# Retention with two heads per pair: products in alternating head order, and head factors by transposes

## The chip, the cores and the metric

The kernel runs on one core of one Trainium2 chip. The metric is device time in microseconds (us) from launch to end; lower is better. A core has TensorE (PE, matrix products; its weight loads are shown as PEld), VectorE (DVE), ScalarE (ACT), GpSimd (POOL) and SyncE (SP, which here issues nearly all DMA transfers). TensorE reads SBUF and writes PSUM, which has eight banks.

## The reference, cut to what matters

Two layers, each a token mixer with four branches (retention, short convolution, Fourier, pooling) and then a SwiGLU block, on 256 latent tokens; layer 0 also carries 256 context tokens as a second stream. Everything is float32. The part that the change touches is the retention, with 4 heads of 64 features:

```python
scores = jnp.einsum('bhid,bhjd->bhij', qc, kc) * intra[None]
out = (jnp.einsum('bhij,bhjv->bhiv', scores, vc)
       + jnp.einsum('bhid,bhdv->bhiv', qc, state) * q_decay)
state = state * chunk_decay + jnp.einsum('bhjd,bhjv->bhdv', kc * k_decay, vc)
...
mu = jnp.mean(y, axis=-1, keepdims=True)
var = jnp.mean(jnp.square(y - mu), axis=-1, keepdims=True)
y = (y - mu) * lax.rsqrt(var + EPS)
```

It runs forward and backward over the tokens; the context's final states are the start states of the latent stream. Each head's output is normalized over its 64 features and multiplied by a gate.

## The kernel before

All large projections are done in three float32r products per block (`mm3`, L208 to L212: high part times high part, and the two mixed ones). The weights come block by block through SyncE's queue; ScalarE copies the high part of each (L105) and VectorE subtracts it to get the low part (L115). The schedule is written out by hand: a list of steps is run in order, and after a step that holds a block, `tick` (L216) lets up to two of the queued side jobs go on by one `yield`. Retention is such a side job: TensorE works on a projection, then does one small burst for retention, then goes on with the next projection.

`retention(c)` (L741) handles the pair of heads 2c and 2c+1, for c = 0 and then c = 1, once in each layer: four times in all. Head j of the pair has its 64 features in partitions `off[j]`, 0 to 63 or 64 to 127. Its stages, one burst on TensorE each:

- L749, L750: SyncE loads `qd` (decay factors of q) and `dm` (decay masks).
- L753, `ktp`: the context's keys are transposed, 2 transposes per pair.
- L766 to L775, `st`: the states at the end of the context; per head two products of 128 rows, 64 columns and 128 moving columns into the head's half of one PSUM bank.
- L783 to L792, `scores`: per head two products of 64 rows (the head's features) and 256 moving columns into a bank of its own; then VectorE multiplies by the mask (`am`, L791).
- L799 to L804, `heads`: `py`, one bank, where head j writes partitions `off[j]`. Two products per head with `am` (128 rows, 64 columns), and for the latent stream (`s == 0`) two more with the states (`st` times `qd`, 64 rows, 64 columns).
- L806, L807: ScalarE squares `py`, VectorE multiplies it by the gate.
- L810 to L821, `variance`: VectorE and POOL make the norm's factor per token and head, and VectorE copies it out to 64 columns per head (`rx`, L820).
- L827, `normed`: `rx` (tokens by features) is brought to features by tokens by a float32 product with the identity, two per stream; VectorE multiplies (L829), and ScalarE and VectorE split the result into high and low part for the gates' products.

In layer 0 (NS = 2) scores and heads run first for the context (s = 1), then for the latent stream (s = 0); layer 1 has s = 0 alone. So the program has four `st` sets, six `scores` sets, two `heads` sets without states (s = 1) and four with (s = 0). In the program, each set lists all products of head 0 and then all of head 1. The banks of tag "a" that these stages use go round in order (L177).

Of the kernel before, what the change touches and what calls it, by code (L numbers as in the profile page):

```python
# [12 lines left out]
ALU = mybir.AluOpType  # L13
# [4 lines left out]
P = 128  # L18
D = 1024
KC = D // P  # L20
SEQ = 256
MIX = 256
HEADS = 4
DH = 64
# [135 lines left out]
def kernel(ctx: ExitStack, tc: tile.TileContext, a: dict, out: bass.AP):  # L160
    ctx.enter_context(tc.manual_schedule())
    nc = tc.nc
# [14 lines left out]
    def bank(tag, name, shape=None, keep=False):  # L177

        i = banks[tag].pop(0)
        if not keep:  # L180
            banks[tag].append(i)
        t = psum.tile([P, 512], F32, tag=f"bank{i}", name=name)
        return t if shape is None else cut(t, shape)
# [4 lines left out]
    def cut(t, shape):  # L188
        n = 1
        for x in shape:  # L190
            n *= x
        t = t[:, :n]
        if len(shape) == 2:
            t = t.rearrange("p (a b) -> p a b", b=shape[1])
        if len(shape) == 3:
            t = t.rearrange("p (a b c) -> p a b c", b=shape[1], c=shape[2])
        return t

    def load(pl, shape, src, name, eng=None, **kw):
        t = pl.tile(shape, F32, name=name, **kw)  # L200
        (eng or nc.sync).dma_start(t, src)
        return t

    def split(hi, lo, src):
        nc.scalar.activation(hi, src, AF.Copy)
        nc.vector.tensor_tensor(lo, src, hi.bitcast(F32), op=ALU.subtract)
# [24 lines left out]
    ident = load(cst, [P, P], a["c_ident"], "ident", nc.scalar)  # L231
# [375 lines left out]
    def mixer(l, h, hnext, start=None):  # L607
# [8 lines left out]
        def rt(tag, shape, name, bufs=1):  # L616
            n = 1
            for x in shape:
                n *= x
            return cut(P_["t"].tile([P, n], F32, tag=tag, name=name, bufs=bufs), shape)  # L620
# [5 lines left out]
        vt = []  # L626
# [105 lines left out]
        def both():  # L732
            yield from retention(0)
            yield
            yield from retention(1)

        def vrow(i, hh, at, dims):
            row = vscr[i][l * HEADS + hh : l * HEADS + hh + 1, 0:1]
            return bass.AP(row.tensor, row.offset + at, dims)

        def retention(c):  # L741

            kT, qT, gs, kt = qk["k", c], qk["q", c], qk["g", c], fix["kt"]
            off = [slice(j * DH, (j + 1) * DH) for j in range(2)]
            qd = rt("qd", [2, SEQ], f"qd{l}{c}")
            dm = [rt(f"dm{j}", [2, SEQ], f"dm{l}{c}{j}") for j in range(2)]
            for j in range(2):
                for d in range(2):
                    nc.sync.dma_start(qd[off[j], d, :], vrow(0, 2 * c + j, 257 * (1 - d), [[0, DH], [1, SEQ]]))  # L749
                nc.sync.dma_start(dm[j], vrow(1, 2 * c + j, 1, [[1, P], [P, 2], [1, SEQ]]))  # L750
            pt = bank("a", f"ktp{l}{c}", [2, P])
            for t in range(2):
                nc.tensor.transpose(pt[:, t, :], kT[:, (t + 2) * P : (t + 3) * P], ident)  # L753
            nc.scalar.activation(kt[:, :, c * P : (c + 1) * P], pt, AF.Copy)
            vd = rt("vd", [2, 2, 2 * DH], f"vd{l}{c}")
            for t in range(2):
                for d in range(2):
                    nc.vector.tensor_tensor(
                        vd[:, t, :, d * DH : (d + 1) * DH],
                        vt[1][:, t, 2 * c : 2 * c + 2, :],  # L760
                        kdec[:, l, t, d, 2 * c : 2 * c + 2].unsqueeze(2).to_broadcast([P, 2, DH]),
                        op=ALU.mult,
                    )
            yield
            pst = bank("a", f"st{l}{c}", [2 * DH])
            for j in range(2):  # L766
                hh = 2 * c + j
                for t in range(2):
                    nc.tensor.matmul(
                        pst[off[j], :],  # L770
                        lhsT=kt[:, t, hh * DH : (hh + 1) * DH],
                        rhs=vd[:, t, j, :],
                        start=(t == 0),
                        stop=(t == 1),
                    )  # L775
            st = rt("st", [2 * DH], "st")
            nc.scalar.activation(st, pst, AF.Copy)
            nc.vector.tensor_tensor(qd, qd, qT[:, :SEQ].unsqueeze(1).to_broadcast([P, 2, SEQ]), op=ALU.mult)

            def scores(s):  # L780
                sl = slice(s * SEQ, (s + 1) * SEQ)
                am = []
                for j in range(2):  # L783
                    pss = bank("a", f"sc{l}{c}{s}{j}", [2, SEQ])
                    for jt in range(2):
                        lo = s * SEQ + jt * P
                        nc.tensor.matmul(
                            pss[:, jt, :], lhsT=kT[off[j], lo : lo + P], rhs=qT[off[j], sl], start=True, stop=True
                        )
                    m = rt("am", [2, SEQ], "am", 3)  # L790
                    nc.vector.tensor_tensor(m, pss, dm[j][:, :, ::-1], op=ALU.mult)  # L791
                    am.append(m)  # L792
                return am

            def heads(s, am):
                sl = slice(s * SEQ, (s + 1) * SEQ)
                py = bank("a", f"y{l}{c}{s}")[:, :SEQ]
                n = 4 if s == 0 else 2
                for j in range(2):  # L799
                    todo = [(vt[s][:, jt, 2 * c + j, :], am[j][:, jt, :]) for jt in range(2)]  # L800
                    if s == 0:
                        todo += [(st[off[j], d * DH : (d + 1) * DH], qd[off[j], d, :]) for d in range(2)]
                    for i, (lhs, rhs) in enumerate(todo):
                        nc.tensor.matmul(py[off[j], :], lhsT=lhs, rhs=rhs, start=(i == 0), stop=(i == n - 1))  # L804
                ys = rt("ys", [2, SEQ], "ys", 2)
                nc.scalar.activation(ys[:, 0, :], py, AF.Square)  # L806
                nc.vector.tensor_tensor(ys[:, 1, :], py, gs[:, sl], op=ALU.mult)  # L807
                return ys

            def variance(s, ys):  # L810
                pv = bank("a", f"var{l}{c}{s}", [2, 2])
                for t in range(2):
                    nc.tensor.matmul(
                        pv[:, t, :], lhsT=ys[:, 0, t * P : (t + 1) * P], rhs=bsel, start=True, stop=True
                    )
                ms = sm.tile([P, 4], F32, tag="vms", name="vms")
                nc.vector.tensor_scalar(ms, pv.rearrange("p a b -> p (a b)"), EPS, None, op0=ALU.add)
                nc.gpsimd.tensor_tensor(ms, ms, mhalf, op=ALU.pow)
                rx = rt("rx", [4, DH], "rx", 2)
                nc.vector.tensor_copy(rx, ms.unsqueeze(2).to_broadcast([P, 4, DH]))  # L820
                return rx.rearrange("p a d -> p (a d)")  # L821

            def normed(s, ys, rx):
                pr = bank("a", f"yr{l}{c}{s}")[:, :SEQ]
                for t in range(2):
                    ts = slice(t * P, (t + 1) * P)
                    nc.tensor.matmul(pr[:, ts], lhsT=rx[:, ts], rhs=ident, start=True, stop=True)  # L827
                gy = ys[:, 1, :]
                nc.vector.tensor_tensor(gy, gy, pr, op=ALU.mult)  # L829
                sl = slice(s * SEQ, (s + 1) * SEQ)  # L830
                split(br[0][0][c][:, sl], br[0][1][c][:, sl], gy)

            yield
            am = {}
            for s in range(NS - 1, -1, -1):
                am[s] = scores(s)
                yield
                am[s] = heads(s, am[s])
                yield
            rx = {s: variance(s, am[s]) for s in am}  # L840
            yield
            for s in am:
                normed(s, am[s], rx[s])
# [589 lines left out]
    start = next(i for i, st in enumerate(mix0) if st.tick)  # L1433
# [123 lines left out]
```

## Time and profile before

| | us |
|---|---|
| median of 3 runs | 1261.3 (1260.61 to 1261.71) |
| profiled execution, as timed | 1262.2 |
| its span, first to last instruction | 1260.3 |
| TensorE busy in the span | 1222.6 (97%) |
| VectorE busy | 776.7 (62%) |
| ScalarE busy | 454.1 (36%) |
| POOL busy | 41.1 (3%) |

How to read it: the rows further down come from one profiled execution, so sums are made against its span. A float32 product shows as two matmul records (two passes), a float32r product and a transpose as one. Matmuls are pipelined and the ends of their records are modelled, so records overlap; the cost of a burst is read from the chain of waits or from start to start. "a\*b" in a matmul's row is its rows and columns in the array.

### The profile page before, as it was taken

What the parts mean: (1) busy time and instruction counts of PE and PEld (TensorE: products, weight loads), DVE (VectorE), ACT (ScalarE), POOL (GpSimd) and SP (SyncE); (2) the same over time, 40 slices, a digit from 0 to 9 for tenths busy, and PEclk for the clock granted to TensorE, in tenths of its full rate; (3) what the DMA queues carried; (4) which work ended last, traced back from release to release, by engine and by line L of the source; (5) the groups of instructions that cost most, each with busy time, mean ns of one, the idle gap of its engine ahead of it and who ended that gap; (6) DMA issues with size and microseconds to landing.
All of it is one profiled execution on the core that took longest, in us unless ns stands there. A gap on an engine that the chain in (4) does not pass through costs nothing.

```text
span 1260.3 us, 17305 instructions
## 1 busy us (share of the span) xinstructions
PE 1222.6 (97%) x6830; PEld 1044.5 (83%) x6830; DVE 776.7 (62%) x1242; ACT 454.1 (36%) x712; POOL 41.1 (3%) x39
## 2 busy tenths in 40 slices
PE   8999999999989989999999999989999999999997
PEld 4687878888878778888888788779889998999986
DVE  4453454399977465997666422475666666666644
ACT  3332332322222363222222222354334455444532
POOL 1500000000000000000000000000000000000000
PEclk9999999999999999999999999999999999999999
DMA  8542322566676424677768733244355564665672
GB/s 294 184 130 69 100 84 101 200 198 225 217 171 137 134 98 123 225 230 234 240 217 205 177 103 101 67 132 134 103 151 168 190 217 134 186 183 185 192 222 88
DMA packets 66434, 206.31 MB, mean 164 GB/s; under 512 B 14640, under 2 KB 18224, under 8 KB 66352
## 3 DMA queue, kind: packets, MB, share of 16 engines
q1 hardware_dynamic: 65200, 204.96, 52.7%
q8 instruction: 54, 0.88, 0.3%
q10 hardware_dynamic: 1152, 0.24, 0.1%
q14 instruction: 28, 0.23, 0.1%
HBM read 204.06 MB, written 1.11 MB: 163 GB/s over the span
## 4 chain that ended last, share of the span: by engine, by line
PE 81%; DVE 8%; ACT 3%; DMA 3%; issue 3%; POOL 0%; SPq 0%; ACTq 0%; DVEq 0%; POOLq 0%
PE up L211 10%; PE up L210 10%; PE up L212 10%; PE gate L210 5%; PE gate L211 5%; PE gate L212 5%; PE dn L212 4%; PE dn L211 4%; PE dn L210 4%; DVE mjunk L320 2%; PE y L804 1%; PE wo L212 1%; PE wo L211 1%; PE wo L210 1%; ACT junk L425 1%
## 5 line engine op out<-in xcount | busy, mean ns | idle before, releaser
L320 DVE SCALAR_TENSOR_TENSOR mjunk<-raw_mod,crow 128x1024 bf16<-128x1024 f32 x128 | 156.4, 1222 | 8.1 <-DMA raw_mod<-in_w_modt 5.5
L211 PE MATMUL up<-hm0lo,hi_up 128*128 128x512 f32 (+1 forms) x384 | 143.2, 373 | 0.4 <-DVE hm0lo L452 0.4
L210 PE MATMUL up<-hm0hi,hi_up 128*128 128x512 f32 (+1 forms) x384 | 143.3, 373 | 0.0
L212 PE MATMUL up<-hm0hi,lo_up 128*128 128x512 f32 (+1 forms) x384 | 143.2, 373 | 0.0
L115 DVE TENSOR_TENSOR lo_up<-raw_up,hi_up 128x1024 fp32r<-128x1024 f32 x88 | 107.5, 1223 | 34.0 <-ACT hi_up L105 34.0
L115 DVE TENSOR_TENSOR lo_gt<-raw_gt,hi_gt 128x1280 fp32r<-128x1280 f32 x64 | 95.3, 1488 | 33.6 <-ACT hi_gt L105 33.5
L115 DVE TENSOR_TENSOR lo_dn<-raw_dn,hi_dn 128x1024 fp32r<-128x1024 f32 x44 | 53.6, 1224 | 89.4 <-ACT hi_dn L105 89.4
L210 PE MATMUL gate<-h0hi,hi_gt 128*128 128x512 f32 x256 | 101.2, 395 | 4.0 <-DVE sg L989 3.9
L105 ACT ACTIVATE hi_gt<-raw_gt 128x1280 fp32r<-128x1280 f32 x64 | 81.1, 1268 | 54.0 <-DMA raw_gt<-in_w_gate 53.8
L211 PE MATMUL gate<-h0lo,hi_gt 128*128 128x512 f32 x256 | 100.4, 392 | 0.0
L210 PE MATMUL up<-hm1hi,hi_up 128*128 128x256 f32 x352 | 100.4, 285 | 0.0
L212 PE MATMUL gate<-h0hi,lo_gt 128*128 128x512 f32 x256 | 100.3, 392 | 0.0
L211 PE MATMUL up<-hm1lo,hi_up 128*128 128x256 f32 x352 | 100.3, 285 | 0.0
L212 PE MATMUL up<-hm1hi,lo_up 128*128 128x256 f32 x352 | 100.1, 284 | 0.0
L105 ACT ACTIVATE hi_up<-raw_up 128x1024 fp32r<-128x1024 f32 x88 | 92.2, 1049 | 14.4 <-DMA raw_up<-in_w_up 13.8
L211 PEld LDWEIGHTS up<-hm0lo,hi_up 128*128 128x128 f32 x384 | 72.9, 190 | 13.0 <-DVE hm0lo L452 0.6
L212 PEld LDWEIGHTS up<-hm0hi,lo_up 128*128 128x128 f32 x384 | 72.8, 190 | 12.7
L210 PEld LDWEIGHTS up<-hm0hi,hi_up 128*128 128x128 f32 x384 | 73.0, 190 | 12.5
L105 ACT ACTIVATE hi_dn<-raw_dn 128x1024 fp32r<-128x1024 f32 x44 | 46.3, 1057 | 93.5 <-PE dn L212 78.4
L210 PE MATMUL gate<-hf0hi,hi_gt 128*128 128x256 f32 x256 | 73.4, 287 | 0.0
L212 PE MATMUL gate<-hf0hi,lo_gt 128*128 128x256 f32 x256 | 72.4, 283 | 0.0
L211 PE MATMUL gate<-hf0lo,hi_gt 128*128 128x256 f32 x256 | 72.4, 283 | 0.0
(330 smaller groups left out, 2749.4 us busy)
## 6 DMA issues: line engine op xcount, KB each, us to landing
raw_up<-in_w_up SPq DMA_DIRECT2D x88, 512.0 KB, 3.9
raw_gt<-in_w_gate SPq DMA_DIRECT2D x64, 640.0 KB, 4.0
raw_mod<-in_w_modt SPq DMA_DIRECT2D x80, 512.0 KB, 4.0
raw_dn<-in_w_down SPq DMA_DIRECT2D x44, 512.0 KB, 3.7
raw_in<-in_w_in SPq DMA_DIRECT2D x28, 512.0 KB, 3.7
raw_mod<-in_w_mod SPq DMA_DIRECT2D x16, 512.0 KB, 4.6
raw_wo<-in_w_o SPq DMA_DIRECT2D x16, 512.0 KB, 4.1
grow<-gscr SPq DMA_DIRECT2D x6, 512.0 KB, 13.0
```

Of the source, the lines that this page charges most:

```text
L105: self.nc.scalar.activation(b.hi, b.raw, AF.Copy)
L115: self.nc.vector.tensor_tensor(b.lo, b.raw, b.hi.bitcast(F32), op=ALU.subtract)
L210: nc.tensor.matmul(ps, lhsT=st[0], rhs=mv[0], start=first, stop=False)
L211: nc.tensor.matmul(ps, lhsT=st[0], rhs=mv[1], start=False, stop=False)
L212: nc.tensor.matmul(ps, lhsT=st[1], rhs=mv[0], start=False, stop=last)
L320: nc.vector.scalar_tensor_tensor(junk, b.raw, 1.0, crow[s], op0=ALU.mult, op1=ALU.mult, accum_out=out()[:, s, i : i + 1])
L425: nc.scalar.activation(junk, src, AF.Square, scale=1.0 / 32.0, accum_out=acc)
L804: nc.tensor.matmul(py[off[j], :], lhsT=lhs, rhs=rhs, start=(i == 0), stop=(i == n - 1))
```

## The change

In three places the loop over the two heads goes inside the loop over their products, so that the products of head 0 and head 1 alternate: the states (`st`), the scores and `heads`. In `scores` both heads' banks are taken before the first product, and both masks are applied after the last. In `heads` the index i runs over the two products with `am` and, for the latent stream, the two with the states. The number of these products, their operands and the order of accumulation within a head stay the same. In `normed` the product with the identity is replaced by TensorE's transpose, as in L753. Nothing else changes.

```diff
             pst = bank("a", f"st{l}{c}", [2 * DH])
-            for j in range(2):
-                hh = 2 * c + j
-                for t in range(2):
+            for t in range(2):
+                for j in range(2):
+                    hh = 2 * c + j
                     nc.tensor.matmul(
                         pst[off[j], :],
...
                 am = []
+                pss = [bank("a", f"sc{l}{c}{s}{j}", [2, SEQ]) for j in range(2)]
+                for jt in range(2):
+                    lo = s * SEQ + jt * P
+                    for j in range(2):
+                        nc.tensor.matmul(
+                            pss[j][:, jt, :], lhsT=kT[off[j], lo : lo + P], rhs=qT[off[j], sl], start=True, stop=True
+                        )
                 for j in range(2):
-                    pss = bank("a", f"sc{l}{c}{s}{j}", [2, SEQ])
-                    for jt in range(2):
-                        lo = s * SEQ + jt * P
-                        nc.tensor.matmul(
-                            pss[:, jt, :], lhsT=kT[off[j], lo : lo + P], rhs=qT[off[j], sl], start=True, stop=True
-                        )
                     m = rt("am", [2, SEQ], "am", 3)
-                    nc.vector.tensor_tensor(m, pss, dm[j][:, :, ::-1], op=ALU.mult)
+                    nc.vector.tensor_tensor(m, pss[j], dm[j][:, :, ::-1], op=ALU.mult)
                     am.append(m)
...
                 n = 4 if s == 0 else 2
-                for j in range(2):
-                    todo = [(vt[s][:, jt, 2 * c + j, :], am[j][:, jt, :]) for jt in range(2)]
-                    if s == 0:
-                        todo += [(st[off[j], d * DH : (d + 1) * DH], qd[off[j], d, :]) for d in range(2)]
-                    for i, (lhs, rhs) in enumerate(todo):
+                for i in range(n):
+                    for j in range(2):
+                        if i < 2:
+                            lhs, rhs = vt[s][:, i, 2 * c + j, :], am[j][:, i, :]
+                        else:
+                            lhs, rhs = st[off[j], (i - 2) * DH : (i - 1) * DH], qd[off[j], i - 2, :]
                         nc.tensor.matmul(py[off[j], :], lhsT=lhs, rhs=rhs, start=(i == 0), stop=(i == n - 1))
...
                     ts = slice(t * P, (t + 1) * P)
-                    nc.tensor.matmul(pr[:, ts], lhsT=rx[:, ts], rhs=ident, start=True, stop=True)
+                    nc.tensor.transpose(pr[:, ts], rx[:, ts], ident)
```

## Rows read from the trace of the kernel before

**Rows 1.** The page, part 1 (busy us, share, instructions) and part 2 (granted clock by slices).

```profile
PE 1222.6 (97%) x6830; PEld 1044.5 (83%) x6830; DVE 776.7 (62%) x1242; ACT 454.1 (36%) x712; POOL 41.1 (3%) x39
...
PEclk9999999999999999999999999999999999999999
```

**Rows 2.** Stretches: length, busy PE, PEld, DVE, ACT, POOL, clock, DMA share, GB/s.

```profile
70.00:215.00 145.00, 145.00 (x703) 114.32 (x703) 72.38 (x124) 43.48 (x68) 4.03 (x4) 1.00 0.32 93
...
250.00:360.00 110.00, 109.89 (x485) 90.67 (x484) 106.83 (x156) 30.47 (x35) 0.00 (x0) 1.00 0.65 205
...
937.00:960.00 23.00, 23.00 (x177) 20.89 (x176) 14.64 (x23) 10.68 (x15) 1.01 (x1) 1.00 0.50 169
```

**Rows 3.** Waits of PE, 885 to 960 us: us in total, times, longest.

```profile
PE yr L827 <- DVE rx L820: 0.9, 1, 0.9
PE st L769 <- ACT pmf L914: 0.7, 1, 0.7
PE y L804 <- DVE am L791: 0.7, 1, 0.7
```

**Rows 4.** Chain of waits, bursts of retention: start us, us on the chain, what, passes.

```profile
88.46 0.59 PE st L769 x8
...
94.76 1.07 PE sc L787 x8
...
101.50 1.02 PE y L804 x8
...
120.11 4.02 PE y L804 x16
...
136.19 0.89 PE yr L827 x8
...
905.37 4.02 PE y L804 x16
...
936.74 4.09 PE y L804 x16
...
948.66 0.45 PE yr L827 x4
```

**Rows 5.** Timeline of PE inside one sixteen-pass set: start us, us, instruction, shapes, count.

```profile
120.04 1.08 PE L804 MATMUL y<-am,v 128*64 128x256 f32 x4
...
120.31 0.38 PE L804 MATMUL y<-am,v 128*64 128x256 f32 x1
...
120.52 0.38 PE L804 MATMUL y<-am,v 128*64 128x256 f32 x1
...
121.05 1.07 PE L804 MATMUL y<-qd,st 64*64 64x256 f32 x4
```

**Rows 6.** Timeline of DVE at three places; in brackets idle time before, and its releaser.

```profile
251.76 0.69 DVE L989 TENSOR_TENSOR sg<-sg,pb 128x512 f32<-128x512 f32 x1 [0.62 <-PE pb L212]
...
903.30 1.28 DVE L791 TENSOR_TENSOR am<-sc,dm 128x512 f32<-128x512 f32 x2
...
936.00 1.28 DVE L791 TENSOR_TENSOR am<-sc,dm 128x512 f32<-128x512 f32 x2
```

**Rows 7.** Lines L753 and L827: records, ns min/median/max, first and last start, shapes.

```profile
L753 PE MATMUL ktp<-ident,k x8: 270/272/273, 82.6 to 921.3; 128*128 128x128 f32 x8
...
L827 PE MATMUL yr<-ident,rx x24: 270/275/348, 136.0 to 948.8; 128*128 128x128 f32 x24
```

**Rows 8.** Timeline of PE around two transposes of L753.

```profile
82.38 0.39 PE L212 MATMUL gps<-h0hi,lo_in 128*128 128x512 f32 x1
82.61 0.38 PE L753 MATMUL ktp<-ident,k 128*128 128x128 f32 x2
...
83.06 0.39 PE L211 MATMUL gps<-h0lo,hi_in 128*128 128x512 f32 x1
```

**Rows 9.** Chain of waits in layer 1, two pieces between 909 and 937 us.

```profile
912.49 0.39 ACT up L887
...
929.04 6.70 DMA dm<-vscr
```

## The prediction

> **What bounds the kernel now.** I read the page first: TensorE is busy for 97% of the span, and its clock is at the full 2.4 GHz level in all 40 slices [rows 1]. So whatever shortens TensorE's own queue should shorten the run, unless another engine ends last in the stage concerned. The stages of the change are the retention of layer 0 (85 to 205 us) and of layer 1 (892 to 949 us). The view by stretches shows TensorE without a gap in 70 to 215 us and in 937 to 960 us, and VectorE almost without one (106.8 of 110 us) in 250 to 360 us [rows 2]. Of TensorE's waits, the three between 885 and 960 us are the ones in the way: 0.9, 0.7 and 0.7 us, all in layer 1 [rows 3]. The chain of waits then gives the price of each burst of products that the diff touches [rows 4]: what stands there is time on the path, since the matmul before a burst and the one behind it are TensorE's too.
>
> **Which bursts are already in pairs.** A float32 product is recorded as two passes. A set of four products, two per head (eight passes of 256 columns), takes 1.07 us for scores and 1.02 us for `y` of the second stream; the eight 128-column passes of `st` take 0.59 us [rows 4]. The `y` set of the first stream has eight products, sixteen passes, and takes 4.02 us, not 2.04 [rows 4]. The timeline shows how: four passes of shape 128\*64, then four of 64\*64 (and the same again for the other head), a quarter 1.01 us from start to start, its passes 0.21 us apart [rows 5]. So four passes cost there what eight cost at 101.50. In the eight-pass sets the passes of head 1 must run beside those of head 0 (one output in PSUM partitions 0 to 63, the other in 64 to 127), though the program lists head 0 first. In the sixteen-pass set the shape changes within each head, and no pair crosses a change of shape.
>
> **`heads` of the first stream (L799 to L804).** With `i` outside and `j` inside, all four 128\*64 products come first, then all four 64\*64. The first half becomes the set that costs 1.02 us at 101.50. For the second half no row shows two 64\*64 products together. Its bounds are 1.02 us (paired like the 128\*64 set; columns, rows and outputs are disjoint) and 2.01 us (the two 64\*64 quarters as they run now). I take 1.02, since `sc` (heads split by rows) and `y` (heads split by columns) both pair. A set then costs 2.04 us and saves 4.02 - 2.04 = 1.98 us; at the other bound, 0.99 us. There are four such sets, two in each layer.
>
> The set also gains an earlier wait: its second product now needs the second `am`, which before only the fifth needed, and head 0's remaining products are queued behind it. VectorE makes both `am` in 1.28 us [rows 6]. In three of the four sets they are done before the set starts (the tightest: 903.30 + 1.28 = 904.58 against 905.37 [rows 4, 6]). In the last one `y` starts at 936.74 and the second `am` ends at 936.00 + 1.28 = 937.28 [rows 4, 6]; with 0.04 us from an `am` to its product that costs 0.58 us (bounds 0, and 0.64 if half of the 1.28 shows). That set saves 1.98 - 0.58 = 1.40 us.
>
> **The other sets (L766, L783, and `heads` of the second stream).** They keep their products, already in pairs, so I take nothing for six `sc`, two `y` and four `st` sets. On the gain side `sc` could at best fall from 1.07 to four passes of 0.21 us, 1.4 us over six sets; on the other side stands the third rival. The first `am` now waits for the third product instead of the second; paired heads end together, so nothing. The bank of head 1 is claimed one product earlier; no wait of TensorE for a bank stands in [rows 3].
>
> **Head factors by transposes (L827).** Twelve products are 24 recorded passes [rows 7], 0.89 us for eight [rows 4], so 0.11 each. The existing transposes at L753 are eight in the program and eight in the trace: one pass each [rows 7]. On the path, two of them cost (83.06 - 82.38) - 2 x 0.23 = 0.22 us, 0.11 each [rows 8]. Layer 0: 4 x 0.11 = 0.44 instead of 0.89, twice: 0.90 us. Layer 1: 0.22 instead of 0.45, 0.23 us twice; but the first of them lies at 916.7 us, where TensorE waits for VectorE [rows 3] and the chain goes on over other engines and a load until 936 [rows 9], so I count only the second, at 948.66: 0.23 us (bounds 0 and 0.46).
>
> **Does a shift of TensorE pass on?** In layer 0 TensorE has no gap up to 215 us [rows 2], so 2 x 1.98 + 0.90 = 4.86 us arrive there. VectorE's full stretch opens with a gate product at 251.76, released by TensorE [rows 6]: it moves with it. In layer 1 the first `y` set ends before the pooling projection, whose end releases ScalarE's `up` at 912.49; from there the chain runs over VectorE, POOL, the split of a gate block and SyncE's queue to the `dm` load (6.70 us) and the `am` at 936.00 [rows 6, 9]. All of it starts from that projection, so it moves by the full 1.98 us, the loads with it, because SyncE's queue waits there for VectorE to free a block. If that chain stood still, the 1.98 us would be lost. With 1.40 us for the second set and 0.23 us for `yr`, layer 1 gives 3.61 us.
>
> Sum: 4.86 + 3.61 = 8.47 us. The profiled execution has a span of 1260.3 us, 1262.2 us as timed; the span would be 1251.8 us. The median of the runs before is 1261.3 us, between the two; the same 8.5 us less is 1252.8 us.
>
> **A rule of the skill against the trace.** The eight-pass sets cost about five steps of 0.21 us, not eight. The Trainium skill (TensorE: Matmul & The Clock Gate, "Part 3: Packing small matmuls") says that matmuls start and end strictly in program order. This trace disagrees: in order, one head after the other, seven steps would follow each other, about 1.5 us, where 1.02 is measured. What this rule would give is the fourth rival. For 64\*64 the Trainium skill (TensorEngine Tiling (Array Packing), "Key Properties") says that different tiles run in parallel; by that the second half pairs and the sum is as above, but no row shows it yet.
>
> **Rivals.** A measurement of this kernel can tell about 0.2%, 2.5 us, from no change.
>
> 1. The 64\*64 half stays serial. Each set saves 0.99 instead of 1.98: 1.98 + 0.90 in layer 0, 0.99 + (0.99 - 0.58) + 0.23 in layer 1, together 4.5 us: 1256.8 us. For it: no such pair in the trace. Against it: the other two shapes pair. 10%.
> 2. The gain of layer 0 is taken back where VectorE is full: if its stretch from 251 us began when it begins now, the 4.86 us would come back as waits for gate blocks, and 3.6 us remain: 1257.7 us. For it: 97% busy there [rows 2]. Against it: its first product there waits for TensorE [rows 6]. 9%.
> 3. Slower: pairs form only while a head's products stand together, and every change of head costs a drain, as every change of shape does now. A quarter takes 1.01 us [rows 5], 4 x 0.21 plus 0.17 for the change. With four changes in a set of four products and nothing paired, 4 x (0.42 + 0.17) = 2.36 us instead of 1.02 to 1.07 in eight sets (+10.4 us); in the `st` sets, with passes of 0.11, 4 x (0.22 + 0.17) = 1.56 instead of 0.59, four times (+3.9); the big sets 8 x 0.59 = 4.72 instead of 4.02 (+2.8); less 1.1 for the transposes: +16.0 us, 1277.3 us. It decides from about 0.7 us more in each of the twelve small sets, which eats the 8.5. Against it: partners start together today although a head's other passes lie between them in the program, so the engine already alternates. The Trainium skill (TensorEngine Tiling (Array Packing), "Key Properties") has the drain for a change of mode, not of tile within one mode; the trace agrees so far that it shows the loss at changes of shape. 6%.
> 4. The small sets are not yet paired as I read them and gain too: 3 x 0.21 us in eight sets, 5.0 us on top: 1247.8 us. The rule on program order would give this; the 1.02 us speaks against it. 3%.
> 5. The change does not do what it says: the sixteen passes stay serial for another reason than the change of shape within a head (their accumulation into one bank), and only the transposes count: 1261.3 - 1.1 = 1260.2 us. For it: the reason is inferred from two sets. 8%.
>
> **How the numbers follow.** The forecast has 64%, with its own spread from 1250.8 (no wait for the second `am`, both `yr` of layer 1, the `sc` bound) to 1254.8 (the shift of layer 1's chain lost). The range takes in rivals 1 and 2 and leaves out 3, 4 and 5: 1250.8 to 1258.2. Faster by over 0.2% (below 1258.8 us): forecast and rivals 1, 2 and 4, 86%; within 0.2%: rival 5, 8%; slower: rival 3, 6%.
>
> **What would show it.** In the chain of waits after, the four `y` sets of the first stream should take 2.0 us each (3.0 under rival 1, 4.0 under 5), the last one some 0.6 us longer; `sc`, `st` and the small `y` sets unchanged at 1.07, 0.59 and 1.02 (2.4 for `sc` under rival 3); `yr` with 12 records instead of 24 and 0.44 us a set in layer 0. VectorE's full stretch should open near 247 us and the `dm` load of layer 1's second pair near 922 us (929.04 less 4.86 and 1.98). The prediction is wrong if `y` falls as said but the span does not follow, or if the small sets change at all.

## The result, and the profile after

The changed kernel takes 1253.07 us (median of 4 runs, 1251.05 to 1253.19), the kernel before 1261.13 us beside it (1260.61 to 1261.71): 8.06 us less, ratio 0.9933, 95% interval 0.9922 to 0.9945. The forecast was 1252.8 us. The profiled execution has a span of 1251.2 us; before it was 1260.3 us.

The page after, part 1 (busy us, share, instructions). It answers to [rows 1]: 13 matmul records fewer, 12 of them the transposes' second passes and one probably missing in the record, and 9.9 us less busy time on TensorE; the other engines work as long as before.

```profile
PE 1212.7 (97%) x6817; PEld 1038.7 (83%) x6818; DVE 777.1 (62%) x1242; ACT 454.3 (36%) x712; POOL 41.1 (3%) x39
```

The chain of waits after, the bursts of retention (start us, us on the chain, what, passes). It answers to [rows 4].

```profile
87.97 0.59 PE st L769 x8
...
94.26 1.06 PE sc L787 x8
...
119.59 2.02 PE y L806 x16
...
133.68 0.44 PE yr L829 x4
...
900.01 2.02 PE y L806 x16
...
929.21 2.69 PE y L806 x16
...
939.73 0.22 PE yr L829 x2
```

The sixteen-pass sets take 2.02 us instead of 4.02, the last one 2.69 instead of 4.09; `st` and `sc` are as long as before (0.59, and 1.06 for 1.07); `yr` takes 0.44 us where it took 0.89. The places can be compared row by row: `st` starts 0.49 us earlier than before, ahead of anything that the change made shorter, so 0.49 us of the profile's 9.1 us is not its work. The lead is 0.52 us at the first large `y` set and 2.51 us at `yr`. It is 5.36 us at layer 1's first `y` set, 7.53 at the second and 8.93 us at the last `yr`.

The timeline of TensorE in the first and in the last of these sets (in brackets: idle before, and its releaser). It answers to [rows 5].

```profile
119.52 1.08 PE L806 MATMUL y<-am,v 128*64 128x256 f32 x8
120.53 1.08 PE L806 MATMUL y<-qd,st 64*64 64x256 f32 x8
121.54 0.50 PE L210 MATMUL fu<-h0hi,hi_in 128*128 128x512 f32 x1
...
929.21 1.67 PE L806 MATMUL y<-am,v 128*64 128x256 f32 x8 [0.70 <-DVE am L792]
930.82 1.08 PE L806 MATMUL y<-qd,st 64*64 64x256 f32 x8
931.83 0.39 PE L210 MATMUL gate<-hf0hi,hi_gt 128*128 128x256 f32 x1
```

Eight passes now take the 1.01 us that four took, in both shapes. In the last set the first half lasts 1.61 us instead of 1.01: that is the wait for the second `am`.

The waits of TensorE in 880 to 960 us after. They answer to [rows 3]: the same three, as long as before, and a new one of 0.2 us, where a product of a gate block (`pb`) waits for ScalarE. The second experiment shows what it comes from.

```profile
PE yr L829 <- DVE rx L822: 0.9, 1, 0.9
PE y L806 <- DVE am L792: 0.7, 1, 0.7
PE st L769 <- ACT pmf L916: 0.7, 1, 0.7
PE pb L210 <- ACT sg L982: 0.2, 1, 0.2
```

The timeline of VectorE after, where its full stretch opens and where the last masks are applied. It answers to [rows 6]: 251.76 has become 246.38.

```profile
246.38 0.69 DVE L991 TENSOR_TENSOR sg<-sg,pb 128x512 f32<-128x512 f32 x1 [0.50 <-PE pb L212]
...
928.48 1.28 DVE L792 TENSOR_TENSOR am<-sc,dm 128x512 f32<-128x512 f32 x2
```

### The profile page after: what moved, and what is told of

It reads as the page before. It is cut to its first block, busy times and chain, and to the rows that moved or that the text cites. A ratio compares the mean times of both kernels' runs of the same rounds, so it can differ in the third digit from the quotient of the medians.

```text
span 1251.2 us, 17280 instructions
## 1 busy us (share of the span) xinstructions
PE 1212.7 (97%) x6817; PEld 1038.7 (83%) x6818; DVE 777.1 (62%) x1242; ACT 454.3 (36%) x712; POOL 41.1 (3%) x39
## 4 chain that ended last, share of the span: by engine, by line
PE 81%; DVE 8%; DMA 3%; issue 3%; ACT 3%; POOL 0%; SPq 0%; DVEq 0%; POOLq 0%; ACTq 0%
PE up L211 10%; PE up L212 10%; PE up L210 10%; PE gate L210 5%; PE gate L211 5%; PE gate L212 5%; PE dn L212 4%; PE dn L211 4%; PE dn L210 4%; DVE mjunk L320 2%; PE wo L211 1%; PE wo L212 1%; PE wo L210 1%; ACT junk L425 1%; PE pb L212 1%
```

## Experiments

The theory: a set of products pairs its heads as long as the shape in the array stays the same; before, only the sixteen-pass sets changed shape within a head. The rivals: the small sets gain or lose too, the alternation itself makes the pairs, a change of shape spoils a set in any order. Each kernel is timed beside the kernel before on its chip: 1261.22 us for the first four, 1261.59 us for the other three.

**The large sets alone.** In `heads`, for the latent stream only:

```diff
-                for j in range(2):
-                    todo = [(vt[s][:, jt, 2 * c + j, :], am[j][:, jt, :]) for jt in range(2)]
...
+                order = [(j, i) for i in range(4) for j in range(2)] if s == 0 else [(j, i) for j in range(2) for i in range(2)]
+                for j, i in order:
```

> The change in `heads` of the latent stream alone; states, scores, the context's `heads` and the identity product stay as before. Theory (all of the gain beside the transposes comes from the four sixteen-pass `y` sets, 4.02 to 2.03 us, less 0.58 us for the second `am` in the last one): 4 x 2.0 - 0.6 = 7.4 us off, 1253.7 us; the last set 2.6 us. Rival (the other sets' order matters too): they stay at 1.07, 0.59 and 1.02 us here, and the time lies nearer to the kernel before than 1253.7 us by whatever they gave.

Measured: 1254.13 us, 7.1 us less (ratio 0.9942, 0.9926 to 0.9959). The chain of waits of this kernel, first and last set:

```profile
120.07 2.02 PE y L806 x16
...
929.97 2.69 PE y L806 x16
```

The chain of waits gives the sets the lengths that were expected; of the 8.1 us these four carry about 7.1, where 7.4 was expected.

**The transposes alone.**

```diff
-                    nc.tensor.matmul(pr[:, ts], lhsT=rx[:, ts], rhs=ident, start=True, stop=True)
+                    nc.tensor.transpose(pr[:, ts], rx[:, ts], ident)
```

> The head factors by transposes alone. Theory: 0.45 us off twice in layer 0 and 0.23 once in layer 1 (the first set of layer 1 lies where TensorE waits for VectorE): 1.1 us off, 1260.0 us; the sets in layer 0 0.44 instead of 0.89 us. Rival (a transpose is no shorter on the path than the two passes): no difference, 1261.1 us.

Measured: 1260.33 us, 0.9 us less (ratio 0.9992, 0.9983 to 1.0001). The interval reaches just past no difference, so the time alone is weak; the lengths on the chain are as expected, 0.44 us in layer 0:

```profile
135.30 0.44 PE yr L827 x4
...
945.84 0.22 PE yr L827 x2
```

Whether the first set of layer 1 counts can be read within one execution. The timeline of TensorE, this kernel first, then the kernel before:

```profile
914.15 0.41 PE L827 MATMUL yr<-ident,rx 128*128 128x128 f32 x2 [0.90 <-DVE rx L820]
...
918.43 0.38 PE L753 MATMUL ktp<-ident,k 128*128 128x128 f32 x2
...
921.87 0.38 PE L210 MATMUL pb<-br,hi_gt 128*128 128x256 f32 x1 [0.21 <-ACT sg L980]
...
923.95 0.97 PE L769 MATMUL st<-vd,kt 128*64 128x128 f32 x8 [0.67 <-ACT pmf L914]
```

```profile
916.66 0.68 PE L827 MATMUL yr<-ident,rx 128*128 128x128 f32 x4 [0.89 <-DVE rx L820]
...
921.20 0.38 PE L753 MATMUL ktp<-ident,k 128*128 128x128 f32 x2
...
926.47 0.97 PE L769 MATMUL st<-vd,kt 128*64 128x128 f32 x8 [0.67 <-ACT pmf L914]
```

From `yr` to `ktp` it is 4.28 us instead of 4.54: 0.26 us are gained. From `yr` to `st` it is 9.80 instead of 9.81: they are given back. Most of it goes into a new wait of 0.21 us on the way, where a `pb` product waits for a gate of ScalarE, which had not become faster; the wait of `st` itself is 0.67 us in both. The forecast left this set out, rightly.

**The small sets alone.** States, scores and the context's `heads` in alternating order, as in the diff; the large sets and L827 as before.

```diff
-                for j in range(2):
-                    pss = bank("a", f"sc{l}{c}{s}{j}", [2, SEQ])
...
+                order = [(j, i) for j in range(2) for i in range(4)] if s == 0 else [(j, i) for i in range(2) for j in range(2)]
+                for j, i in order:
```

> Alternating order in the states, the scores and the context's `heads` alone; the sixteen-pass sets and the identity product stay as before. Theory (these sets ran in pairs already): no difference, 1261.1 us, sets at 1.06, 0.59 and 1.02 us. Rival 3 of the prediction (pairs need a head's products together): sets of over 1.8 us and over 1270 us. Rival 4 (not yet paired before): about 5 us off, 1256 us.

Measured: 1261.47 us (ratio 1.0003, 0.9994 to 1.0013): no difference. The chain of waits:

```profile
88.26 0.59 PE st L769 x8
...
94.55 1.06 PE sc L787 x8
...
101.28 1.01 PE y L807 x8
...
119.88 4.02 PE y L807 x16
```

All are within 0.01 us of [rows 4]. These sets ran in pairs before, in head-by-head order; alternation neither makes pairs nor breaks them. That ends the third and the fourth rival.

**Grouped by shape, not alternating.** The order within the large set is head 0's two `am` products, head 1's two, then head 0's and head 1's state products.

```diff
+                order = [(j, 2 * half + i) for half in range(2) for j in range(2) for i in range(2)] if s == 0 else [(j, i) for j in range(2) for i in range(2)]
+                for j, i in order:
```

> Only the sixteen-pass set is changed: the two `am` products of head 0, the two of head 1, then the two state products of head 0, the two of head 1. Grouped by shape, no alternation. Theory (what kept the pairs apart was the change of shape within a head, and alternation as such is worth nothing): the set falls to 2.0 us as in the full change, 2.6 in the last one, 1253.7 us. Rival (products of the two heads must be neighbours in the program): the set stays at 4.0 us, 1261.1 us.

Measured: 1253.18 us, 8.0 us less (ratio 0.9938, 0.9923 to 0.9952). The chain of waits and the timeline of TensorE:

```profile
120.08 2.04 PE y L806 x16
```

```profile
120.01 1.09 PE L806 MATMUL y<-am,v 128*64 128x256 f32 x8
121.03 1.09 PE L806 MATMUL y<-qd,st 64*64 64x256 f32 x8
...
928.92 1.67 PE L806 MATMUL y<-am,v 128*64 128x256 f32 x8
930.52 1.09 PE L806 MATMUL y<-qd,st 64*64 64x256 f32 x8
```

Head 1's products stand behind all of head 0's of the same shape and still run beside them. Single records show it too: the last two passes of the first half start together, and both are over after the 0.39 us of one.

```profile
120.71 0.39 PE L806 MATMUL y<-am,v 128*64 128x256 f32 x2
```

So what the change repairs is the shape change within a head; the alternation in its name is worth 0.02 us a set (2.04 against 2.02). The rows do not name the head of a pass; the order in the queue is taken from the program. The 0.95 us between this median and that of the first experiment is not the order's either: its sets are no shorter, and the two intervals overlap.

One thing stays open. Before, head 1's `am` products stood eight passes behind head 0's, here four, and no run has partners of one shape eight passes apart, so distance may have parted them as well. That a change of shape is enough by itself is seen before the change: head 0's last state product and head 1's first `am` product are neighbours in the program, and still each quarter takes its own 1.01 us [rows 5].

The last set loses its 0.6 us here too, although head 1's first product is third instead of second in line: after the second `am` all of head 1's passes of this shape are still to run, in either order.

**Alternating, but with three changes of shape instead of one.**

```diff
+                order = [(j, i) for i in (0, 2, 1, 3) for j in range(2)] if s == 0 else [(j, i) for j in range(2) for i in range(2)]
+                for j, i in order:
```

> Only the sixteen-pass set is changed: heads alternate, but an `am` product and a state product of each head follow each other, so that the shape changes after every pair of products, three times in a set instead of once. Theory (pairs form within a shape, each change of shape costs a fixed piece of about 0.15 us): four groups of four passes at about 0.58 us, 2.3 us a set, 4 x 1.7 - 0.6 = 6.2 us off, 1254.9 us. Rival (pairs need a run of products of one shape): groups near 1.0 us, a set of 4.0 us, 1261.1 us.

Measured: 1255.5 us, 6.1 us less (ratio 0.9950, 0.9935 to 0.9965). The chain of waits, then the timeline of TensorE:

```profile
119.62 2.32 PE y L806 x16
```

```profile
119.55 0.65 PE L806 MATMUL y<-am,v 128*64 128x256 f32 x4
120.13 0.65 PE L806 MATMUL y<-qd,st 64*64 64x256 f32 x4
120.71 0.65 PE L806 MATMUL y<-am,v 128*64 128x256 f32 x4
121.29 0.65 PE L806 MATMUL y<-qd,st 64*64 64x256 f32 x4
```

Two more changes of shape cost 2.32 - 2.02 = 0.30 us, 0.15 each. Pairs form between any two changes; what a change costs besides is small. Before, the loss was not the three changes but that between two of them only one head's products stood.

**The states first.** The full change, with the state products ahead of the `am` products in the latent stream, and the full change once more beside it on the same chip.

```diff
-                for i in range(n):
-                    for j in range(2):
...
+                order = [(j, i) for i in (2, 3, 0, 1) for j in range(2)] if s == 0 else [(j, i) for i in range(2) for j in range(2)]
+                for j, i in order:
```

> The full change, but in the latent stream the state products come first and the `am` products last. Theory (in layer 1's second set TensorE waits 0.7 us for the first `am` and 0.6 us for the second, while the operands of the state products lie ready): those waits are covered by the 1.0 us of state products; about 1.0 us off against the full change, 1252.0 us where the full change has 1253.1. Rival (the chain over VectorE sets the end of that stretch anyway): no difference to the full change.

> The full change once more, beside the states-first version on the same chip: 1253.1 us, the last `y` set 2.6 us after a wait of 0.7 us.

Measured: 1251.83 us (1251.08 to 1252.19, 5 runs) for states first, 1252.53 us (1252.29 to 1253.25, 5 runs) for the full change; against the kernel before 0.9922 (0.9910 to 0.9935) and 0.9930 (0.9918 to 0.9943). In this series no run of the one reaches into those of the other, and states first has the lowest median of these kernels; one run of the full change in the first series, 1251.05 us, was as short. The medians are 0.7 us apart where 1.0 was expected. The chain of waits of the states-first kernel, from layer 0's first `y` set, and its timelines of TensorE and VectorE:

```profile
119.83 2.02 PE y L807 x16
...
901.17 2.02 PE y L807 x16
...
929.68 2.39 PE y L807 x16
```

```profile
929.61 1.08 PE L807 MATMUL y<-qd,st 64*64 64x256 f32 x8
930.62 1.45 PE L807 MATMUL y<-am,v 128*64 128x256 f32 x8
```

```profile
929.66 1.28 DVE L792 TENSOR_TENSOR am<-sc,dm 128x512 f32<-128x512 f32 x2
```

The same of the full change beside it:

```profile
120.05 2.02 PE y L806 x16
...
900.49 2.03 PE y L806 x16
...
929.84 2.68 PE y L806 x16
```

```profile
929.84 1.67 PE L806 MATMUL y<-am,v 128*64 128x256 f32 x8 [0.83 <-DVE am L792]
```

From the start of layer 1's first `y` set to the end of its second it is 929.68 + 2.39 - 901.17 = 30.90 us against 929.84 + 2.68 - 900.49 = 32.03: 1.13 us gained at the place itself. The 0.83 us of idle time are gone; of the 0.66 us by which the set was longer than 2.02, 0.37 stay, since the second `am` is ready only at 929.66 + 1.28 = 930.94, after its half has begun at 930.62. That the spans do not show all of it lies elsewhere: from layer 0's first set to layer 1's first this execution took 781.34 us and the other 780.44, over a stretch where the two kernels do the same work in lengths that agree. TensorE's granted clock differs there: from 360 to 430 us its mean was 0.95 for states first and 1.00 for the full change, from 430 to 480 us 0.97 and 0.93, so states first had more time at the lower of the two levels. That this makes the 0.9 us is not shown.

## Why the prediction was right, point by point

**The price of a large set.** Forecast 2.04 us, measured 2.02 (2.04 where grouped by shape). The open term was the second half: two 64\*64 products had never been seen together. It pairs like the others, 1.01 us for eight passes, so the upper bound of 2.01 us and the first rival fell. The fifth rival fell with the same sets: it had them stay at 4.0 us.

**Layer 0.** Forecast 4.86 us by the end of its retention. Measured where VectorE's full stretch opens: 5.38 us, less the 0.49 us that was there from the start, is 4.89 us. Behind that stretch, at layer 1's first `y` set, it is 5.36 - 0.49 = 4.87 us, and in the second profile of the full change 905.37 - 900.49, less 0.03 at the start, 4.85 us. So it passed through: the second rival fell. That the figures behind the stretch agree to 0.02 us is luck. In the third experiment, where no set was shorter by more than 0.01 us, layer 1's first `y` set came 0.99 us later after the first `st` than in the kernel before (906.16 - 88.26 = 817.90 us against 905.37 - 88.46 = 816.91).

**Layer 1's chain.** Between the two `y` sets the forecast let everything move by 1.98 us; the lead grew by 2.17, from 5.36 to 7.53. Up to SyncE's last `dm` load it grew by just 1.98, to 929.04 - 921.70 = 7.34, of which 0.49 were there from the start; the forecast said about 922:

```profile
921.70 0.60 SPq L750 DMA_DIRECT2D dm<-vscr  x1
```

One detail was off without effect: the forecast named that `dm` load as what the masks wait for. In the profile after, the chain of waits goes instead from the `qd` load just before it over VectorE's product, the split of a gate block and two gate operations to the same masks. VectorE's rows, before and then after, show that this was so already: before, it has no idle time from 933.20 to the masks at 936.00, and the `dm` load had landed at 929.04 + 6.70 = 935.74 [rows 9].

```profile
933.20 0.69 DVE L778 TENSOR_TENSOR qd<-qd,q 128x512 f32<-128x512 f32 x1 [3.94 <-DMA qd<-vscr]
```

```profile
925.67 0.69 DVE L778 TENSOR_TENSOR qd<-qd,q 128x512 f32<-128x512 f32 x1 [3.76 <-DMA qd<-vscr]
```

Both loads move with SyncE's queue, so the 1.98 us came through all the same. The other 0.19 us came in at the `qd` load: 933.20 - 925.67 is 7.53 us already. The forecast had nothing for it.

**The second `am`.** Forecast a loss of 0.58 us in the last set; it takes 931.83 - 929.21 = 2.62 us from start to start where the first takes 2.02: 0.60 us. The states-first kernel shows the cause from the other side: with work ahead that needs no mask, the idle time before the set goes, and of this loss 0.37 us are left.

**The transposes.** Forecast 0.90 us in layer 0, and 0.23 us in layer 1 for the second set only. Measured 0.44 us a set of four, one record each (12 records), and the gain of the first set of layer 1 given back within the next 10 us. Their time alone, 0.9 us, is below the 1.1 forecast but its interval holds it.

**What was taken at nothing** was nothing: the third experiment puts the other sets together at 0.25 us slower, with an interval from 0.8 us faster to 1.6 us slower.

The sum is 8.47 us; the median moved by 8.06 us, and by 9.06 us in the second series. The parts add up by themselves too, 7.1 us for the large sets and 0.9 us for the transposes, but that they meet 8.06 so closely is luck: each has an interval of about a microsecond or more to either side, and the large sets grouped by shape gave 8.0 us alone. What carries the account is the length of each set on the chain of waits, not these sums of medians.

Two slips in the prediction changed nothing. Its three gains, 0.58, 0.23 and 1.4 us, put the lower end of the forecast's own spread at 1250.6 us, not 1250.8. And a 9 in the clock's row stands for 90% or more, not for the full clock; the mean granted clock was 0.993 in both profiles, before and after.

**The rule on program order**, from the Trainium skill (TensorE: Matmul & The Clock Gate, "Part 3: Packing small matmuls"), that matmuls start and end strictly in the order of the program, does not hold here: grouped by shape, head 1's products stand four passes behind head 0's in the program, and the set takes the time of pairs all the same.

## What to carry to other kernels

Where two half-array products could run side by side, count what a set costs against its passes before reordering it: a set that already takes half gave nothing more here, in either order. What kept partners apart here is a change of shape (rows by columns in the array) between them, so group products by shape first; up to four passes apart, alternating is optional. A set whose operands arrive late is best begun with the products whose operands are already there.

## What the runs showed of the hardware that was not expected

A change of shape between 128\*64 and 64\*64 costs 0.15 us on the path (two more of them in a set: 2.02 to 2.32 us) and leaves pairing within each shape alone, down to groups of two products. A partner may stand four passes later in the program and still run beside the first: the set ends within 0.02 us of the alternating one (2.04 against 2.02 us). How much further this reaches, no run tested.
